# Three edits around the router of an expert layer: where eight weight loads stand in the queue, where three row scalings stand on VectorE, and forty products that nobody reads

## The chip, the cores and the metric

The kernel runs on one core of one Trainium2 chip. The metric is the device time of one execution in microseconds (us). TensorE is called PE in the rows (PEld is its weight load), VectorE is DVE, ScalarE is ACT, GpSimd is POOL, and SyncE is SP. A "q" behind an engine's name is its sequencer, which issues DMAs and takes branches.

## The reference

The model is a small float32 network of two parts. The first part has two layers. Each is a mixer (neighbourhood attention and an mLSTM in layer 0, grouped attention in layer 1) followed by a mixture of experts; a second part of two other layers follows. The change lies in the mixture of experts, which the reference computes as:

```python
scores = sigmoid(h @ router_w)                      # (N, 16)
sel = (scores + router_b).reshape(N, 4, 4)
g_idx = argmax(top_k(sel, 2)[0].sum(-1), -1)        # best group of four experts
e_idx = ...                                         # the best two experts inside that group
w = w / w.sum(-1)                                   # their scores, normalised
for e in range(16):
    y = y + comb[:, e:e+1] * ((silu(h @ w1[e]) * (h @ w3[e])) @ w2[e])
```

N is 512 tokens in layer 0 (256 latent and 256 context rows) and 256 tokens in layer 1; the width is 1024, an expert's inner width 512.

## The kernel before

**Products.** Each float32 weight is split in two numbers that PE multiplies faster: ACT copies it to a rounded `wh` (L90) and DVE subtracts to get the rest `wl` (L91). A product of weights and tokens is then three matmuls, `wh·xh`, `wl·xh`, `wh·xl` (L105 to L107). There are three buffers of `wh` and of `wl`, so these splits can run at most three pieces ahead of PE. An expert is 12 pieces of 512 KB: eight for w1 and w3, four for w2.

**Router.** While the mixer's last products run, `Routes.half` (L992 to L1011) transposes the tokens (L164), multiplies them with the router's weights (L1006), takes squares on ACT (L1009) and multiplies the tokens by rows `scales` on DVE (L1011), which gives the token rows `xT`. `moe` (L1404) then decides on DVE, in some thirty small operations that end with `both` (L1490, kept as `decided`): for each token, which two experts it goes to. PE sums `both` over the tokens (L1499: counts before each token); from these DVE makes `q` (L1503, places of the first expert's tokens) and `hot` (L1506, one 128 x 128 table of ones and zeros for each tile of 128 tokens, 4 tiles in layer 0 and 2 in layer 1).

**Token rows.** `rows_out(t)` (L1443 to L1448) makes the scaled rows of tile t on DVE (L1446, 128 x 1024) and has POOL store them to memory (`hd`). The first expert doesn't wait for that memory: PE multiplies the rows with `hot` (L1523), which puts the first expert's tokens in their places, and ACT and DVE split the sum in `xh` and `xl` (L156, L157). All later experts fetch their tokens from `hd` with an indirect DMA from POOL (`gather`, L1608) by the index `idx`, which DVE computes (L1676, L1677) from products of `slotb` and `rk` (L1544, L1546). A gathered tile is transposed by PE (L164) and split again. The factors of the tokens are summed by PE as well (L1709, from `wsr` and `slotb`), while the first expert runs.

**Weight places.** SP issues all weight loads, in order (L1569). Places for pieces are of four kinds: `rawm` (own buffers of `moe`, 16 in layer 0 and 17 in layer 1), `raw` (8, shared with the rest of the kernel), `rawr` (6, over the memory of `xT`), and in layer 1 `more` (2). Pieces are consumed in the order in which the places stand. The last argument but one of `moe` (`late`) names the `rawm` buffers that come behind `raw` in that order:

```python
late, early = [own[i] for i in late], [u for i, u in enumerate(own) if i not in late]
turn = [*(lambda u=u: u for u in more), *early, *[c.raw] * c.RAW, *late]
```

In layer 0 `late` is empty, in layer 1 it is (0, 1, 2, 3, 4). Each load on SP also waits for the one eight loads ahead of it.

**What sets the order.** Each engine works its instructions off in a fixed order, which a scheduler lays out when the kernel is built: by data, buffers and its own estimate of when an operand is there. `tc.issue_after(x)` keeps an instruction behind another one in that order; `split_w` (L73 to L92) is placed with high priority. Behind the first expert's start stands a branch that all engines take (L1327, L1328: the rare case that an expert has more than 128 tokens).

Of the kernel before, what the change touches and what calls it, by code (L numbers as in the profile page):

```python
# [13 lines left out]
AF = mybir.ActivationFunctionType  # L14
ALU = mybir.AluOpType
# [3 lines left out]
P = 128  # L19
# [7 lines left out]
class Core:  # L27
# [108 lines left out]
    def lin_feat2_halves(self, x, w):  # L136


        banks = [[self.acc().rearrange("p (j t) -> p j t", j=2) for _ in range(2)] for _ in range(2)]
        for half, j in ((0, 0), (0, 1), (1, 0), (1, 1)):  # L140
            rows = w[half * 512:(half + 1) * 512, j * 512:(j + 1) * 512]
            for k0, h, l in self.chunks(rows, 512):
                for i in range(4):
                    for k in range(2):
                        a = (h[:, k, i * P:(i + 1) * P], l[:, k, i * P:(i + 1) * P])
                        kk = 4 * half + k0 + k
                        self.mm3(banks[j][i // 2][:, i % 2, :], a, [v[:, kk, :] for v in x], i % 2 == 0 and kk == 0,
                                 kk == KD - 1)
            if half:
                yield j, banks[j]  # L150
# [11 lines left out]
    def transpose(self, out, in_):  # L162
        n = in_.partition_size() if hasattr(in_, "partition_size") else in_.shape[0]
        self.nc.tensor.transpose(out, in_, self.ident[:n, :n])  # L164

    def rsqrt_small(self, out, ms, n):

        self.nc.gpsimd.tensor_tensor(out, ms, self.mhalf[:, :n], op=ALU.pow)


class Stats:
# [24 lines left out]
    def settle(self):  # L196

        c, nc = self.c, self.c.nc
        for x in self.put_off:
            self.gather(x)  # L200
        for i, sq in self.sq.items():
            half = sq[:, :256]
            if sq.shape[1] > 256:
                last = nc.vector.tensor_tensor(half, half, sq[:, 256:], op=ALU.add)
            for t in range(2):
                nc.tensor.matmul(self.tot[:, i + t:i + t + 1], half[:, t * P:(t + 1) * P], c.ones[:, 0:1],
                                 start=self.fresh, stop=True, skip_group_check=True)
                self.fresh = False
                self.left[i + t] = 0
        self.put_off, self.sq = [], {}  # L210
        return last
# [720 lines left out]
class Routes:  # L932
# [64 lines left out]
    def half(self, t, j, bank):  # L997

        c, nc = self.c, self.c.nc
        x, r = self.segs[t // 2]  # L1000
        at = slice(t % 2 * P, t % 2 * P + P)
        for i in range(4):
            c.transpose(bank[:, i * P:(i + 1) * P], x[:, 4 * j + i, at])
        for i in range(4):
            k = 4 * j + i
            nc.tensor.matmul(self.lg[:, t * NE:(t + 1) * NE], x[:, k, at], self.rwB[:, r, k, :], start=t == k == 0,  # L1006
                             stop=k == KD - 1, skip_group_check=True)
        sq = c.const.tile([P, 512], F32, name="sq", tag="sq", bufs=3)
        nc.scalar.activation(sq, bank, AF.Square, accum_out=self.ss[:, t, j:j + 1])  # L1009
        v = lambda a: a.rearrange("t (p j) -> t p j", j=KD)  # L1010
        nc.vector.tensor_tensor(self.turned(self.xT[t], j), v(bank), v(self.scales[r][j]), op=ALU.mult)  # L1011

# [391 lines left out]
def moe(c, s, L, segs, mods, routes, yd, later, slots, late, more=()):  # L1404
# [3 lines left out]
    nc, tc, ins = c.nc, c.tc, c.ins  # L1408
# [11 lines left out]
    slot = mc[:, NE + 12:NE + 12 + P]  # L1420
# [19 lines left out]
    hd = c.dram.tile([T, D], F32, name=f"hd{L}")  # L1440
    xts = [s.tile([P, D], F32, name="xt", tag=tag) for tag in ("ye", "fhl" if nt > 2 else "xg0", "xg0", "xg1")[:nt]]

    def rows_out(t):  # L1443
        r = segs[t // 2][1]
        with tc.issue_after(decided):
            nc.vector.scalar_tensor_tensor(xts[t], routes.xT[t], rstd[:, t:t + 1], routes.shifts[r], op0=ALU.mult,  # L1446
                                           op1=ALU.add)
        nc.gpsimd.dma_start(hd[t * P:(t + 1) * P, :], xts[t])  # L1448
# [39 lines left out]
    g16 = lambda a: a.rearrange("p t (g e) -> p (t g) e", g=4)  # L1488
    fgb = fg.rearrange("p h b -> p (h b)").unsqueeze(2).to_broadcast((P, nt * 4, 4))
    decided = nc.vector.scalar_tensor_tensor(g16(both), rank, 1.5, fgb, op0=ALU.is_lt, op1=ALU.mult).ins  # L1490
    rows_out(0)
    for k in range(2):
        nc.vector.scalar_tensor_tensor(g16(oh[:, k]), rank, float(k), fgb, op0=ALU.is_equal, op1=ALU.mult)


    pp = c.ps()
    for t in range(nt + 1):
        for j in range(min(t + 1, nt)):
            nc.tensor.matmul(pp[:, t * NE:(t + 1) * NE], ub if j == t else ob, both[:, j, :], start=j == 0,  # L1499
                             stop=j == min(t, nt - 1), skip_group_check=True)  # L1500

    q0 = s.tile([P, nt], F32, name="q0")
    nc.vector.scalar_tensor_tensor(q0, pp[:, 0:nt * NE:NE], 1.0, both[:, :, 0], op0=ALU.add, op1=ALU.mult)  # L1503
    hot = s.tile([P, nt, P], F32, name="hot", tag="mtf")
    for t in range(nt):
        nc.vector.tensor_scalar(hot[:, t, :], slot, 1.0, q0[:, t:t + 1], op0=ALU.add, op1=ALU.is_equal)  # L1506
    for t in range(1, nt):
        rows_out(t)

    over = s.tile([P, 2], F32, name="over")  # L1510
    nc.vector.tensor_reduce(over[:, 0:1], pp[:, nt * NE:(nt + 1) * NE], axis=AX.X, op=ALU.max)
# [3 lines left out]
    xh, xl = (s.tile([P, KD, P], F32R, name=n, tag=n) for n in ("xh", "xl"))  # L1515
# [5 lines left out]
    for t in range(nt):  # L1521
        for k in range(KD):
            nc.tensor.matmul(pss[k // 4][:, k % 4 * P:(k % 4 + 1) * P], xts[t][:, k * P:(k + 1) * P], hot[:, t, :],  # L1523
                             start=t == k % 4 == 0, stop=t == nt - 1, skip_group_check=True)
# [17 lines left out]
    for n, (k, t) in enumerate((k, t) for k in range(2) for t in range(nt)):  # L1542
# [4 lines left out]
                         stop=n == 2 * nt - 1, skip_group_check=True)  # L1547
# [155 lines left out]
    for e in range(NE):  # L1703
        f, last = up(e, x, f)
        if e == 0:
            pw = c.ps()
            for a in range(2):
                for n, (b, k, t) in enumerate(sb):
                    nc.tensor.matmul(pw[:, :NE], b, wsr[:, a, k, t], start=a == n == 0, stop=a == 1 and n == 2 * nt - 1,  # L1709
                                     skip_group_check=True)  # L1710
# [10 lines left out]
        if e == NE - LATE:  # L1721
            rows_back()
            which = spare([P, LATE, T], F32R, "which")
            for i in range(LATE):
                for t in range(nt):
                    nc.vector.tensor_scalar(which[:, i, t * P:(t + 1) * P], slot, float(P * t), lastt[:, i:i + 1],
                                            op0=ALU.add, op1=ALU.is_equal)
# [18 lines left out]
    st = Stats(c)  # L1746
    banks = []
    with tc.issue_after(done[0].ins):
# [6 lines left out]
        for k in range(KD):  # L1755
# [5 lines left out]
            ps = banks[k]  # L1761
            for i, (x, r) in enumerate(segs):
                nc.vector.scalar_tensor_tensor(x[:, k, :], ps[:, 256 * i:256 * i + 256], mods.col(5, k, r), x[:, k, :],
                                               op0=ALU.mult, op1=ALU.add)
# [271 lines left out]
def program(tc, ins, out):  # L2036
    nc = tc.nc
    with ExitStack() as ctx:
        c = Core(tc, ctx, ins)
        xl = c.act.tile([P, KD, 256], F32, name="xl")  # L2040
        with ExitStack() as b1:
            c.b1 = b1.enter_context(c.tmp_pool(name="b1"))
            xc = c.b1.tile([P, KD, 256], F32, name="xc", tag="xc")
            with c.tmp_pool(name="even") as s:
# [14 lines left out]
                mods = [Mods(c, 0), Mods(c, 1)]  # L2059
# [22 lines left out]
                bank = lambda: c.st_p.tile([P, 512], F32, name="ada", tag="st")  # L2082
# [10 lines left out]
                B = lambda L: mods[L].scale("B", 4, gains[L][:, 8:16])  # L2093
                routes, yd = even_mixer(c, s, h, nMr, gq, xl, xc, mods[0], lambda: B(0), ada, first_w, made)
            with c.tmp_pool(name="moe0") as s:
                st = moe(c, s, 0, [(xc, 1), (xl, 0)], mods[0], routes, yd, False, 16, ())
            A = mods[1].scale("A", 1, gains[1][:, 0:8])
            with c.tmp_pool(name="odd") as s:
                routes, yd = odd_mixer(c, s, xl, xc, st, mods[1], A, lambda: B(1), ada)
            with c.tmp_pool(name="moe1") as s:  # L2100
                more = c.b1.tile([P, 2, 2, 512], F32, name="more", tag="xc")
                st = moe(c, s, 1, [(xl, 0)], mods[1], routes, yd, True, 17, (0, 1, 2, 3, 4), [more[:, i] for i in range(2)])
        xs = block2_consts(c, ctx.enter_context(c.tmp_pool(name="const2")))
        c.held = scaled(c, xs, xl, c.n1[:, 0, :], range(KD))[5:1:-2] + [c.early]
        for L in range(2):
            w = {n: ins[n][L] for n in W2}
            w["cols"], w["qkg"] = ins[f"cols_{L}"], ins[f"qkg_{L}"]
            xs, st = block2_layer(c, L, xl, xs, w, st, out if L == 1 else None)
# [31 lines left out]
```

## Time and profile before

| | us |
|---|---|
| median of 3 runs | 2318.12 (2313.27 to 2326.68) |
| the profiled execution | 2316.98 |
| its span, first to last instruction | 2315.2 |
| PE busy | 2222.4 (96%) |
| DVE busy | 1789.7 (77%) |
| ACT busy | 1505.2 (65%) |
| POOL busy | 152.3 (7%) |
| mean granted clock of PE | 0.982 |
| moved from memory | 498.39 MB |

A busy PE is not a PE at its peak, and idle time of an engine that isn't the bottleneck costs nothing. The expert layer of layer 0 starts at about 411 us of the span, that of layer 1 at about 904 us.

### The profile page before, as it was taken

What the parts mean: (1) busy time and instruction counts of PE and PEld (TensorE: products, weight loads), DVE (VectorE), ACT (ScalarE), POOL (GpSimd) and SP (SyncE); (2) the same over time, 40 slices, a digit from 0 to 9 for tenths busy, and PEclk for the clock granted to TensorE, in tenths of its full rate; (3) what the DMA queues carried; (4) which work ended last, traced back from release to release, by engine and by line L of the source; (5) the groups of instructions that cost most, each with busy time, mean ns of one, the idle gap of its engine ahead of it and who ended that gap; (6) DMA issues with size and microseconds to landing.
All of it is one profiled execution on the core that took longest, in us unless ns stands there. A gap on an engine that the chain in (4) does not pass through costs nothing.

```text
span 2315.2 us, 37957 instructions
## 1 busy us (share of the span) xinstructions
PE 2222.4 (96%) x14089; PEld 1887.8 (82%) x14089; DVE 1789.7 (77%) x2817; ACT 1505.2 (65%) x2398; POOL 152.3 (7%) x202
## 2 busy tenths in 40 slices
PE   8999999889999998999999999999999999999999
PEld 5665657767777667777778899999999899999997
DVE  4334743789989775899888999778976899867984
ACT  4333442478877453788776999656765999755773
POOL 0020000111110100111101100000000100000000
PEclk9999979899999999999999999999999999999999
DMA  8577603899993745999946545656666645656653
GB/s 303 170 242 279 204 26 118 312 347 366 365 336 142 270 167 207 377 398 348 325 148 204 177 136 150 190 182 183 194 201 185 184 139 146 186 178 183 192 184 117
DMA packets 206204, 507.24 MB, mean 219 GB/s; under 512 B 22711, under 2 KB 32335, under 8 KB 206008
## 3 DMA queue, kind: packets, MB, share of 16 engines
q1 hardware_dynamic: 196728, 490.08, 63.1%
q0 software_dynamic: 9280, 14.62, 1.7%
q8 instruction: 114, 1.87, 0.3%
q14 instruction: 82, 0.67, 0.1%
HBM read 498.39 MB, written 25.19 MB: 226 GB/s over the span
## 4 chain that ended last, share of the span: by engine, by line
PE 51%; DVE 10%; issue 8%; ACT 6%; DMA 3%; POOL 1%; DVEq 0%; SPq 0%; ACTq 0%; POOLq 0%
PE acc L106 15%; PE acc L107 15%; PE acc L105 14%; DVE wl L91 6%; ACT wh L90 3%; PE ps L164 2%; ACT cp L592 1%; DMA raw<-in_exp_w 1%; DMA rawm<-in_exp_w 1%; PE ps L1903 1%; DMA rawr<-in_exp_w 1%; ACT mtf L1635 1%; PE ps L451 0%; PE acc L1894 0%; DVE conf L597 0%
## 5 line engine op out<-in xcount | busy, mean ns | idle before, releaser
L91 DVE TENSOR_TENSOR wl<-raw,wh 128x1024 fp32r<-128x1024 f32 (+2 forms) x520 | 616.1, 1191 | 240.8 <-ACT wh L90 236.4
L90 ACT CAST wh<-raw 128x1024 fp32r<-128x1024 f32 (+2 forms) x520 | 532.1, 1026 | 356.1 <-PE acc L106 187.4
L106 PE MATMUL acc<-hl,wh 128*128 128x256 f32 (+1 forms) x1568 | 450.0, 287 | 0.3 <-DVE hl L916 0.3
L107 PE MATMUL acc<-hh,wl 128*128 128x256 f32 (+1 forms) x1568 | 450.0, 287 | 0.0
L105 PE MATMUL acc<-hh,wh 128*128 128x256 f32 (+1 forms) x1568 | 449.1, 287 | 0.7 <-ACT hh L913 0.6
L105 PEld LDWEIGHTS acc<-hh,wh 128*128 128x128 f32 x1568 | 295.5, 189 | 11.7 <-issue 4.2
L106 PEld LDWEIGHTS acc<-hl,wh 128*128 128x128 f32 x1568 | 295.9, 189 | 7.0 <-issue 2.5
L107 PEld LDWEIGHTS acc<-hh,wl 128*128 128x128 f32 x1568 | 294.9, 188 | 5.8 <-issue 1.3
L91 DVE TENSOR_TENSOR wl<-rawm,wh 128x1024 fp32r<-128x1024 f32 x210 | 250.9, 1219 | 17.6 <-ACT wh L90 14.2
L90 ACT CAST wh<-rawm 128x1024 fp32r<-128x1024 f32 x210 | 218.1, 1052 | 48.8 <-PE acc L107 45.9
L106 PE MATMUL acc<-wl,xh 128*128 128x512 f32 x512 | 211.5, 413 | 16.4 <-DVE wl L91 16.1
L105 PE MATMUL acc<-wh,xh 128*128 128x512 f32 x512 | 202.0, 399 | 6.3 <-PEq L1328 6.3
L107 PE MATMUL acc<-wh,xl 128*128 128x512 f32 x512 | 202.5, 395 | 0.0
L105 PE MATMUL acc<-bh,wh 128*128 128x256 f32 x640 | 178.6, 279 | 0.7 <-ACT bh L273 0.7
L106 PE MATMUL acc<-bl,wh 128*128 128x256 f32 x640 | 178.7, 279 | 0.4 <-DVE bl L274 0.4
L107 PE MATMUL acc<-bh,wl 128*128 128x256 f32 x640 | 178.7, 279 | 0.0
L592 ACT ACTIVATE cp<-ap,col 128x256 f32<-128x256 f32 x368 | 164.7, 506 | 6.4 <-DVE conf L597 6.4
L106 PE MATMUL acc<-wl,hh 128*128 128x512 f32 (+1 forms) x384 | 145.4, 379 | 2.2 <-DVE wl L91 1.9
L105 PE MATMUL acc<-wh,hh 128*128 128x512 f32 (+1 forms) x384 | 147.1, 383 | 0.0
L106 PEld LDWEIGHTS acc<-wl,xh 128*128 128x128 f32 x512 | 97.1, 190 | 60.6 <-DVE wl L91 41.0
L107 PE MATMUL acc<-wh,hl 128*128 128x512 f32 (+1 forms) x384 | 144.6, 377 | 0.0
L106 PEld LDWEIGHTS acc<-bl,wh 128*128 128x128 f32 x640 | 121.1, 189 | 0.8 <-DVE bl L274 0.8
(493 smaller groups left out, 4514.4 us busy)
## 6 DMA issues: line engine op xcount, KB each, us to landing
rawm<-in_exp_w SPq DMA_DIRECT2D x210, 512.0 KB, 6.9
raw<-in_w_in SPq DMA_DIRECT2D x152, 512.0 KB, 3.6
raw<-in_exp_w SPq DMA_DIRECT2D x96, 512.0 KB, 7.0
raw<-in_ada_w SPq DMA_DIRECT2D x80, 512.0 KB, 5.1
raw<-in_w_up SPq DMA_DIRECT2D x80, 512.0 KB, 3.7
rawr<-in_exp_w SPq DMA_DIRECT2D x66, 512.0 KB, 7.0
raw<-in_w_down SPq DMA_DIRECT2D x44, 512.0 KB, 4.4
raw<-in_even_w_in SPq DMA_DIRECT2D x24, 512.0 KB, 5.1
```

The lines of the kernel that those rows point to most:

```text
L90: nc.scalar.copy(h[:, :, :n], raw[:, :, :n])
L91: self.splits.append(nc.vector.tensor_tensor(l[:, :, :n], raw[:, :, :n], h[:, :, :n], op=ALU.subtract).ins)
L105: nc.tensor.matmul(out, a[0], b[0], start=start, stop=False, skip_group_check=True)
L106: nc.tensor.matmul(out, a[0], b[1], start=False, stop=False, skip_group_check=True)
L107: return nc.tensor.matmul(out, a[1], b[0], start=False, stop=stop, skip_group_check=True)
L164: self.nc.tensor.transpose(out, in_, self.ident[:n, :n])
L592: nc.scalar.activation(p[:, i, :], src[:, i, :], AF.Copy, scale=wv)
L1635: nc.scalar.activation(v, a, AF.Tanh, scale=0.5)
L1903: nc.tensor.matmul(po[:, :256], v[:, b, g0 * P:(g0 + 1) * P], pT[:, b].rearrange("p t q -> p (t q)"), start=b == 0, stop=b == 3)
```

## The change

There are three edits. First, layer 0 calls `moe` with `late` = (13, 14, 15): SP then loads 13 `rawm` pieces, the 8 `raw` pieces, the 3 other `rawm` pieces and the 6 `rawr` pieces, where it loaded 16, 8 and 6 before. Second, the scalings of token tiles 1 and up (`rows_out`) must come behind the last `hot` (`marked`), where they had to come behind `both` before. Third, PE gets 20 float32 products of the identity with itself, into a bank that nobody reads, placed behind the last square of the router's statistics; this holds for both layers.

```diff
+    def keep_on(self, n):
+        ps = self.ps("idle")
+        for _ in range(n):
+            self.nc.tensor.matmul(ps[:, :P], self.ident, self.ident, start=True, stop=True, skip_group_check=True)
...
-        nc.scalar.activation(sq, bank, AF.Square, accum_out=self.ss[:, t, j:j + 1])
+        self.seen = nc.scalar.activation(sq, bank, AF.Square, accum_out=self.ss[:, t, j:j + 1]).ins
...
-    def rows_out(t):
+    def rows_out(t, after):
         r = segs[t // 2][1]
-        with tc.issue_after(decided):
+        with tc.issue_after(after):
...
-    rows_out(0)
+    rows_out(0, decided)
...
+    with tc.issue_after(routes.seen):
+        c.keep_on(20)
     pp = c.ps()
...
     for t in range(nt):
-        nc.vector.tensor_scalar(hot[:, t, :], slot, 1.0, q0[:, t:t + 1], op0=ALU.add, op1=ALU.is_equal)
+        marked = nc.vector.tensor_scalar(hot[:, t, :], slot, 1.0, q0[:, t:t + 1], op0=ALU.add, op1=ALU.is_equal).ins
     for t in range(1, nt):
-        rows_out(t)
+        rows_out(t, marked)
...
-                st = moe(c, s, 0, [(xc, 1), (xl, 0)], mods[0], routes, yd, False, 16, ())
+                st = moe(c, s, 0, [(xc, 1), (xl, 0)], mods[0], routes, yd, False, 16, (13, 14, 15))
```

Lines of the changed kernel are 6 higher behind `keep_on` and 8 higher from L1500 on; the names of lines below are those of the kernel before.

**VectorE, layer 0, from `both` on.** Before:

```order
L1490 SCALAR_TENSOR_TENSOR both<-rank,fg 128x64
L1446 SCALAR_TENSOR_TENSOR xt<-xT,route,shifts 128x1024
L1493 SCALAR_TENSOR_TENSOR oh<-rank,fg 128x64 x2
L1503 SCALAR_TENSOR_TENSOR q_3459<-ps,both 128x4
L1446 SCALAR_TENSOR_TENSOR xt<-xT,route,shifts 128x1024
L1506 TENSOR_SCALAR hot<-mc,q_3459 128x128 x4
L1446 SCALAR_TENSOR_TENSOR xt<-xT,route,shifts 128x1024 x2
L1511 TENSOR_REDUCE over<-ps 128x1
L1529 TENSOR_TENSOR rk<-oh,mc 128x8x16
L1512 TENSOR_SCALAR over<-over 128x1
```

and now:

```order
L1496 SCALAR_TENSOR_TENSOR both<-rank,fg 128x64
L1452 SCALAR_TENSOR_TENSOR xt<-xT,route,shifts 128x1024
L1499 SCALAR_TENSOR_TENSOR oh<-rank,fg 128x64 x2
L1511 SCALAR_TENSOR_TENSOR q_3480<-ps,both 128x4
L1519 TENSOR_REDUCE over<-ps 128x1
L1514 TENSOR_SCALAR hot<-mc,q_3480 128x128 x4
L1452 SCALAR_TENSOR_TENSOR xt<-xT,route,shifts 128x1024 x3
L1520 TENSOR_SCALAR over<-over 128x1
L1537 TENSOR_TENSOR rk<-oh,mc 128x8x16
```

The four `hot` (L1506, now L1514) stand ahead of tile 1's scaling (`xt`) and behind one small operation (`over`); the other three scalings follow in one piece.

**VectorE, layer 0, the stretch that ends with `idx`.** It begins behind the split of the first expert's tokens (`xl`, L157). Before, the first row here is the first weight split (`wl`, L91) behind `xl`:

```order
L91 TENSOR_TENSOR wl<-rawm,wh 128x1024
L1544 TENSOR_SCALAR slotb<-mc,pk 128x128 x3
L1555 TENSOR_TENSOR den<-wk 128x4
L91 TENSOR_TENSOR wl<-rawm,wh 128x1024
L1556 RECIPROCAL den<-den 128x4
L91 TENSOR_TENSOR wl<-rawm,wh 128x1024
L1557 TENSOR_TENSOR wk<-wk,den 128x8
L1676 TENSOR_SCALAR none<-ps 128x32
L91 TENSOR_TENSOR wl<-rawm,wh 128x1024
L1558 TENSOR_TENSOR ws<-oh,wk 128x128
L91 TENSOR_TENSOR wl<-rawm,wh 128x1024
L1677 SCALAR_TENSOR_TENSOR idx<-ps,none 128x32
```

and now, where two weight splits and two pairs of `slotb` stand between `xl` and the first row here:

```order
L91 TENSOR_TENSOR wl<-rawm,wh 128x1024
L1552 TENSOR_SCALAR slotb<-mc,pk 128x128
L1563 TENSOR_TENSOR den<-wk 128x4
L91 TENSOR_TENSOR wl<-rawm,wh 128x1024
L1564 RECIPROCAL den<-den 128x4
L1684 TENSOR_SCALAR none<-ps 128x32
L1565 TENSOR_TENSOR wk<-wk,den 128x8
L91 TENSOR_TENSOR wl<-rawm,wh 128x1024 x2
L1566 TENSOR_TENSOR ws<-oh,wk 128x128
L91 TENSOR_TENSOR wl<-rawm,wh 128x1024
L1569 TENSOR_TENSOR wsr<-ws,wsr 128x128
L1685 SCALAR_TENSOR_TENSOR idx<-ps,none 128x32
```

Between `xl` and `idx` there are seven weight splits now, and five before, and the second half of `wsr` has come ahead of `idx`. In layer 1 there are five where there were three.

**ScalarE, layer 0, from the ninth expert's Tanh (`mtf`, L1635) to the tenth's.** Before:

```order
L1635 ACTIVATE mtf<-acc 128x128x4
L90 CAST wh<-rawm 128x1024 x3
L156 CAST xh<-ps 128x512
L90 CAST wh<-rawm 128x1024
L156 CAST xh<-ps 128x512
L90 CAST wh<-rawm 128x1024 x3
L1662 ACTIVATE ye<-acc,wsl 128x512 x2
L90 CAST wh<-raw 128x1024 x2
L159 ACTIVATE fhl<-ps 128x512
L90 CAST wh<-raw 128x1024 x2
L1635 ACTIVATE mtf<-acc 128x128x4
```

and now:

```order
L1643 ACTIVATE mtf<-acc 128x128x4
L90 CAST wh<-rawm 128x1024 x4
L156 CAST xh<-ps 128x512 x2
L90 CAST wh<-raw 128x1024 x3
L1670 ACTIVATE ye<-acc,wsl 128x512
L90 CAST wh<-raw 128x1024
L1670 ACTIVATE ye<-acc,wsl 128x512
L90 CAST wh<-raw 128x1024 x3
L159 ACTIVATE fhl<-ps 128x512
L90 CAST wh<-raw 128x1024
L1643 ACTIVATE mtf<-acc 128x128x4
```

Before, the splits of the gathered tokens (`xh`) come apart from each other in this stretch, as they do in all later experts; now they still stand together, as in the experts ahead of it, and come apart one expert later.

On PE, the 20 products stand in layer 0 between the last router products (L1006) and the first sum of `both` (L1499); in layer 1 18 stand there, and two among the last transposes of the router's tokens. The sums of the factors (L1709) all stand ahead of the first gathered tile's transposes now (16 in layer 0, 8 in layer 1), where half of them stood behind these before. POOL's order is unchanged.

## Rows read from the trace of the kernel before

**Rows 1.** The page: the chain of waits that ended last, by engine

```profile
PE 51%; DVE 10%; issue 8%; ACT 6%; DMA 3%; POOL 1%; DVEq 0%; SPq 0%; ACTq 0%; POOLq 0%
```

**Rows 2.** Timeline, PE, layer 0 (start us, us, operation, [idle before <-what ended it])

```profile
417.15 0.19 PE L1499 MATMUL ps<-both,ub 128*128 128x16 bf16 x1 [6.16 <-DVE both L1490]
...
420.17 9.82 PE L1523 MATMUL ps<-hot,xt 128*128 128x128 f32 x64 [2.48 <-DVE hot L1506]
...
445.16 1.38 PE L164 MATMUL ps<-ident,xg 128*128 128x128 f32 x8 [2.11 <-DMA xg<-hd,idx]
...
447.91 0.77 PE L105 MATMUL acc<-wh,xh 128*128 128x512 f32 x1
```

**Rows 3.** Timeline, DVE, layer 0

```profile
418.55 1.28 DVE L1446 SCALAR_TENSOR_TENSOR xt<-xT,route,shifts 128x1024 f32<-128x1024 f32 x1
419.75 0.96 DVE L1506 TENSOR_SCALAR hot<-mc,q 128x128 f32<-128x128 f32 x4
...
430.65 0.69 DVE L157 TENSOR_TENSOR xl<-ps,xh 128x512 fp32r<-128x512 f32 x1
...
438.95 0.18 DVE L1677 SCALAR_TENSOR_TENSOR idx<-ps,none 128x32 int32<-128x32 f32 x1
```

**Rows 4.** Timeline, PE, layer 1

```profile
912.66 5.78 PE L1523 MATMUL ps<-hot,xt 128*128 128x128 f32 x32 [2.82 <-DVE hot L1506]
...
933.33 1.44 PE L164 MATMUL ps<-ident,xg 128*128 128x128 f32 x8 [2.64 <-DMA xg<-hd,idx]
...
935.28 0.77 PE L105 MATMUL acc<-wh,xh 128*128 128x512 f32 x1
```

**Rows 5.** Windows, the products with `hot` alone: busy us (records), clock

```profile
420.20:424.80 4.60, 4.60 (x22) 4.60 (x23) 0.50 1.00 382
425.50:429.50 4.00, 4.00 (x39) 4.00 (x38) 1.00 1.02 419
```

**Rows 6.** Timeline, DVE, layer 1

```profile
919.10 0.69 DVE L157 TENSOR_TENSOR xl<-ps,xh 128x512 fp32r<-128x512 f32 x1 [0.20 <-ACT xh L156]
...
924.12 0.18 DVE L1677 SCALAR_TENSOR_TENSOR idx<-ps,none 128x32 int32<-128x32 f32 x1
```

**Rows 7.** Waits of SP from 360 to 520 us: total, times, longest

```profile
SPq L1569 <- DVE route L1018: 43.1, 1, 43.1
```

**Rows 8.** Windows with the share of the DMA engines

```profile
380.00:408.00 28.00, 0.45 (x2) 1.00 0.01 1
440.00:450.00 10.00, 4.05 (x3) 0.79 0.78 265
920.00:930.00 10.00, 3.40 (x3) 1.00 1.03 415
```

**Rows 9.** Timeline, SP: loads before and behind the branch, layer 0

```profile
421.51 10.91 SPq L1569 DMA_DIRECT2D rawr<-in_exp_w  x6
444.74 16.34 SPq L1569 DMA_DIRECT2D rawm<-in_exp_w  x16
```

**Rows 10.** Timeline, POOL: the first gather of layer 0, then of layer 1

```profile
439.97 1.10 POOL L1608 DMA_INDIRECT xg<-hd,idx  x1 [5.10 <-DVE lastt L1679]
...
925.08 1.43 POOL L1608 DMA_INDIRECT xg<-hd,idx  x1 [2.67 <-DVE idx L1677]
```

**Rows 11.** Timeline, ACT: Tanh of four experts, the eighth to the eleventh

```profile
576.86 1.12 ACT L1635 ACTIVATE mtf<-acc 128x512 f32<-128x512 f32 x1
...
595.44 1.12 ACT L1635 ACTIVATE mtf<-acc 128x512 f32<-128x512 f32 x1
...
612.89 1.13 ACT L1635 ACTIVATE mtf<-acc 128x512 f32<-128x512 f32 x1 [0.26 <-PE acc L107]
...
632.86 1.13 ACT L1635 ACTIVATE mtf<-acc 128x512 f32<-128x512 f32 x1 [0.68 <-PE acc L107]
```

**Rows 12.** The page: weight splits on DVE, busy us, mean ns | idle before

```profile
L91 DVE TENSOR_TENSOR wl<-rawm,wh 128x1024 fp32r<-128x1024 f32 x210 | 250.9, 1219 | 17.6 <-ACT wh L90 14.2
```

**Rows 13.** The branch's line, PE's own row: both layers, duration ns min/median/max

```profile
L1328 PEldq COMPARE_BRANCH  x2: 333/3310/6288, 469.2 to 959.2; - x2
```

## The prediction

> **What bounds the kernel.** I read the chain of waits on the page first. PE holds 51% of it and DVE and ACT 16%; DMA holds 3% and "issue" 8% [rows 1]. Weight loads are thus hardly ever what ends last, and a shorter load phase alone is worth little. The change touches the start of the two expert layers, so next I read the timelines of PE and DVE there. In layer 0 PE waits three times before its second expert: 6.16 us until the router has decided, 2.48 us until `hot` is there, and 2.11 us for the first gathered tile [rows 2]. The first of these waits stays: the router's arithmetic on DVE isn't touched. So at most the waits behind it, and the products that run slowly behind them, can shrink, and whatever shrinks must get past the gather.
>
> **Edit 2, `hot` ahead of the scalings.** In layer 0 `hot` begins 1.20 us behind the start of tile 1's scaling [rows 3]. That goes, less about 0.1 us for one small operation now ahead of it. The products with `hot` start at about 419.1 instead of 420.17. They don't wait for the scalings: tile 3 is scaled by about 419.6 + 3 x 1.20 = 423.2 us, and PE comes to it only behind three quarters of its records. Layer 1 is alike: 912.66 becomes about 911.5 [rows 4].
>
> **Edit 3, products without a reader.** Behind PE's idle time the products with `hot` began at a granted clock of 0.50, which is 1.2 GHz: 22 records in 4.60 us, 0.209 us each; at 1.00 (2.4 GHz) 39 ran in 4.00 us, 0.103 us each [rows 5]. These are float32 products of 128 x 128, as the new ones are, and come as two records each (32 products in layer 0, 64 records). So the 20 new ones are 40 records: 40 x 0.103 = 4.1 us at full clock, 40 x 0.209 = 8.4 us at half. PE is free at 417.15 - 6.16 = 411.0 us; they end at 415.1, or 419.4 at worst. The first lies under the wait for the router and costs nothing; the second would hold up the sums of `both` by 2.3 us. I take the first, since the clock fell only during the idle time. But PE then still idles 2 us before the sums and another 1.4 us before `hot`, so they need not keep the clock. If it stays full, the 64 products take 64 x 0.103 = 6.6 us for 9.82, and the first expert starts 1.1 + 3.2 = 4.3 us earlier; if it falls as before, 1.1 us. In layer 1, 32 x 0.103 = 3.3 for 5.78, thus 1.2 to 3.7 us; two of the new products stand among the router's transposes there and may cost 4 x 0.103 = 0.4 us.
>
> **What is late next: the gather.** PE waits for it already [rows 2, 4], and nothing in the edits brings it forward by itself. It is released by `idx`, on a DVE that works in order, and there the order has become worse: seven weight splits instead of five stand between `xl` and `idx` in layer 0, five instead of three in layer 1. A split there takes its turn when PE frees a buffer. From the end of `xl` (430.65 + 0.69) to `idx` (438.95) five splits and the small operations took 7.61 us, 1.52 us for each [rows 3]. Seven are 10.65 us. With `xl` 1.1 to 4.3 us earlier, `idx` starts at 437.7 to 440.9: between 1.3 us earlier and 1.9 us later than before; the middle is 0.3 later. In layer 1 three took 4.33 us [rows 6], 1.44 each; five are 7.2 us, with `xl` 1.2 to 3.7 us earlier, so 0.8 earlier to 1.7 later, middle 0.4 later. The first expert's gain is thus spent on DVE's order.
>
> **Behind the gather.** From the first gathered tile's transposes to the next weight product PE took 2.75 us in layer 0, where eight sums of factors stood between, and 1.95 us in layer 1, where four did [rows 2, 4]. These move ahead, into PE's wait, so 0 to 0.8 us are gained in layer 0 and 0 to 0.3 in layer 1; I take 0.4 and 0.2.
>
> **Edit 1, eight loads earlier.** SP waited 43.1 us, until DVE had read the last scale rows, on a `rawm` load [rows 7], and all that time the DMA engines were idle: share 0.01 at 380 to 408 us [rows 8]. The eight `raw` pieces (4 MB, about 10 us at 415 GB/s) now go there. PE doesn't wait for them, so the direct gain is nothing. What they trigger: the six `rawr` loads, which SP could issue only over 421.51 to 432.42 us because each waits for the load eight ahead, are out by about 426 us, when the branch's own operand is ready. SP is then past the branch 12.3 us later (432.42 to 444.74 before [rows 9]), at about 438, and issues loads into the `rawm` places that the first expert has freed. Before, the gather of layer 0 met a queue that ran dry: 439.97 to the transposes at 445.16, 5.2 us [rows 2, 10], with a DMA share of 0.78 at 440 to 450 us [rows 8]. In layer 1, with a share of 1.03 around the gather, the same took from 925.08 to 933.33, 8.25 us [rows 4, 8, 10]. So the gather of layer 0 costs 0 to 3.06 us more. I take the middle, 1.5: the loads start just before the gather, not well before it as in layer 1.
>
> The Trainium skill says in "DMA: Bandwidth & Descriptors" (Issuing engines are not separate DMA queues) that DMAs of all issuing engines run on the same 16 DMA engines and interleave. By that POOL's gather has no lane of its own beside SP's loads, which speaks against this edit; the two gathers just named, 5.2 and 8.25 us, agree. By that rule alone the full 3.06 us would be the value and the time 1.5 us longer.
>
> **The splits' order.** From the tenth expert on, `xh` of the gathered tokens comes in two parts, and an expert takes 632.86 - 612.89 = 19.97 us, where the ninth took 595.44 - 576.86 = 18.58 [rows 11]. In the changed order this switch comes one expert later in layer 0: 1.4 us gained. In layer 1 it stays.
>
> **Sum.** Layer 0: 0.3 - 0.4 + 1.5 = +1.4 us, bounds -1.3 - 0.8 = -2.1 and 1.9 + 3.06 = +5.0. Switch: -1.4. Layer 1: 0.4 - 0.2 + 0.2 = +0.4, bounds -1.1 and +2.1. In all +0.4 us, bounds -4.6 and +5.7. The profiled execution took 2316.98 us (span 2315.2 and 1.8 around it), 1.1 us under the median of the three runs. 2317.4 by that execution, 2318.5 by the median: I forecast 2318 us. A change under 0.5%, 11.6 us, can't be told from none here.
>
> **Rivals.**
>
> *The gain carries through* (0.15). DVE has slack before `idx`, and the seven splits take less than 1.52 us each because PE starts them earlier, at full clock: at 1.22 us, their own length [rows 12], they are 8.5 us and `idx` comes about 3.4 us earlier in layer 0 and 1.9 in layer 1, with the gather as before. With the switch and the sums -8 us, 2310 us. For it: PE's waits for the first gathered tiles are short. Against: the splits were paced by PE, not by their length.
>
> *The branch moves* (0.15). PE stood still for 6.3 us at the branch in layer 0 and 0.3 us in layer 1 [rows 13], for no data. The new products shift all PE instructions behind them. If the stall in layer 0 goes, that is -6 us, 2312 us (0.10). If layer 1 gets one, +6, 2324 us (0.05). The branch is the same code in both layers, which speaks for chance; that nothing else in the row differs speaks for no change. The Trainium skill, in "Runtime: NRT & Kernel Launch" (Instruction fetch mechanics), says that a taken branch whose target isn't in the instructions already loaded waits for a DMA. By that rule the stall would depend on where the code lies, as this rival has it; no row here shows where it lies.
>
> *Slower: the gather behind the loads* (0.15). SP passes the branch by 438 us and fills the queues, and the gather of layer 0 lands in 8.25 us or more while `idx` comes 1.9 us later. This decides if the clock falls again, so that the first expert starts only 1.1 us earlier. Price: the upper bound, +5.7 us, 2323 us.
>
> *The new products don't do what they say* (0.05). They run at half clock and hold up the sums of `both` by 2.3 us in layer 0: with the rest 2320 us.
>
> **Chances.** My forecast, within 4 us of 2318, has 0.50. All single cases lie within 0.5%; faster than that needs two of them at once (gain carried and stall gone, -14, 2304 us), slower needs the late gather with a new stall (+12, 2330 us). With the spread of the runs I say 0.15 faster, 0.77 same, 0.08 slower. Range 2307 to 2327 us; the forecast's own is 2313 to 2323.
>
> **What would show it.** Right: the products with `hot` begin 1.1 us behind their old distance from `both`; `idx` starts within 2 us of its old distance from `both`; the first gather takes over 5.2 us in layer 0, with a DMA share near 1; PE's wait for the first gathered tile is longer than 2.1 us. The 40 records should end before the sums of `both`. Wrong: the second expert starts over 3 us earlier, measured from `both`, in either layer; the stall at the branch comes or goes; PE waits for weight pieces.

## The result and the profile after

The changed kernel takes 2332.52 us (median of 10 runs, 2323.12 to 2344.74), the kernel before 2314.46 us (10 runs, 2308.36 to 2326.68). The ratio is 1.0079, 95% interval 1.0056 to 1.0103: slower by 13 to 24 us, where I had forecast 2318 us and no change. The profiled execution took 2328.57 us. Three lines of its page:

```profile
span 2326.8 us, 38107 instructions
PE 2234.8 (96%) x14169; PEld 1899.0 (82%) x14169; DVE 1791.7 (77%) x2817; ACT 1505.3 (65%) x2398; POOL 152.7 (7%) x202
PE 39%; issue 7%; DVE 7%; ACT 5%; POOL 1%; DMA 0%; DVEq 0%; ACTq 0%; POOLq 0%
```

The span is 11.6 us longer than before. PE is busy 12 us longer, 11 of them with the new products (6.07 us in layer 0 and 5.04 in layer 1), which mostly lie in what were waits. Where the time went is read from the Tanh of the experts on ACT (start, length), here those of the first three experts of layer 0 and of the second and third of layer 1. Before:

```profile
437.65 1.12 ACT L1635 ACTIVATE mtf<-acc 128x512 f32<-128x512 f32 x1
457.24 1.12 ACT L1635 ACTIVATE mtf<-acc 128x512 f32<-128x512 f32 x1
484.18 1.12 ACT L1635 ACTIVATE mtf<-acc 128x512 f32<-128x512 f32 x1
...
943.42 1.10 ACT L1635 ACTIVATE mtf<-acc 128x512 f32<-128x512 f32 x1
965.49 1.15 ACT L1635 ACTIVATE mtf<-acc 128x512 f32<-128x512 f32 x1
```

and after (lines are 8 higher):

```profile
431.63 1.13 ACT L1643 ACTIVATE mtf<-acc 128x512 f32<-128x512 f32 x1
454.88 1.11 ACT L1643 ACTIVATE mtf<-acc 128x512 f32<-128x512 f32 x1
485.68 1.12 ACT L1643 ACTIVATE mtf<-acc 128x512 f32<-128x512 f32 x1
...
948.61 1.10 ACT L1643 ACTIVATE mtf<-acc 128x512 f32<-128x512 f32 x1
976.06 1.12 ACT L1643 ACTIVATE mtf<-acc 128x512 f32<-128x512 f32 x1
```

From the second to the third Tanh, layer 0 took 26.9 us and takes 30.8, layer 1 took 22.1 and takes 27.5: +3.9 and +5.4 us, four fifths of the loss in two stretches. Both contain the branch. PE's own row of the branch, which read 333 and 6288 ns before [rows 13], is now:

```profile
L1334 PEldq COMPARE_BRANCH  x2: 5928/6018/6107, 465.8 to 964.4; - x2
```

So layer 1 has a wait of 6.1 us where it had 0.3. In layer 0 the wait was there before; what is new is a second one just behind it, 1.99 us (last row below). PE's timeline of layer 0 after, with what answers to [rows 2]:

```profile
408.32 6.07 PE L170 MATMUL idle<-ident 128*128 128x128 f32 x40
...
415.62 7.38 PE L1531 MATMUL ps<-hot,xt 128*128 128x128 f32 x64 [0.89 <-DVE hot L1514]
...
445.27 1.94 PE L164 MATMUL ps<-ident,xg 128*128 128x128 f32 x8 [7.23 <-DMA xg<-hd,idx]
...
471.86 0.77 PE L107 MATMUL acc<-wh,fhl 128*128 128x512 f32 x1 [5.73 <-PEq L1334]
...
477.18 0.79 PE L105 MATMUL acc<-wh,xh 128*128 128x512 f32 x1 [1.99 <-ACT wh L90]
```

The first expert does start sooner: counted from `both` on DVE (416.87 before, 413.38 after) the products with `hot` begin 2.2 us later instead of 3.3, and take 7.38 instead of 9.82 us, 3.5 us gained (of these, 2.4 us were this execution's clock, as two later traces show). All of it goes into the wait for the first gathered tile, 7.23 us for 2.11. DVE, POOL and SP show why (answering to [rows 3], [rows 10], [rows 9] and [rows 7]):

```profile
413.38 0.22 DVE L1496 SCALAR_TENSOR_TENSOR both<-rank,fg 128x64 bf16<-128x64 f32 x1
...
436.33 0.18 DVE L1685 SCALAR_TENSOR_TENSOR idx<-ps,none 128x32 int32<-128x32 f32 x1
```

```profile
437.35 1.27 POOL L1616 DMA_INDIRECT xg<-hd,idx  x1 [5.00 <-DVE idx L1685]
```

```profile
410.16 6.24 SPq L1577 DMA_DIRECT2D raw<-in_exp_w  x8
...
423.15 11.15 SPq L1577 DMA_DIRECT2D rawr<-in_exp_w  x6
445.13 12.58 SPq L1577 DMA_DIRECT2D rawm<-in_exp_w  x13
```

```profile
SPq L1577 <- DVE route L1024: 46.7, 1, 46.7
```

`idx` comes 22.95 us behind `both` instead of 22.08, and its gather takes 7.9 us to PE's transposes (437.35 to 445.27) instead of 5.2. SP's rows hold a surprise: the eight `raw` loads were not moved into the idle time. SP still waited 46.7 us for the scale rows ahead of them, now at the eleventh load and not at the fourteenth; the changed `moe` takes the three late places from memory first, so the eleventh to thirteenth place, not the late ones, came to lie over the scale rows. The share of the DMA engines at 380 to 408 us is 0.00.

### The profile page after: what moved, and what is told of

Read it like the earlier page. It is cut to its first block, busy times and chain, and to the rows that moved or that the text cites. A ratio compares the mean times of both kernels' runs of the same rounds, so it can differ in the third digit from the quotient of the medians.

```text
span 2326.8 us, 38107 instructions
## 1 busy us (share of the span) xinstructions
PE 2234.8 (96%) x14169; PEld 1899.0 (82%) x14169; DVE 1791.7 (77%) x2817; ACT 1505.3 (65%) x2398; POOL 152.7 (7%) x202
## 3 DMA queue, kind: packets, MB, share of 16 engines
q8 instruction: 115, 1.88, 0.3%
## 4 chain that ended last, share of the span: by engine, by line
PE 39%; issue 7%; DVE 7%; ACT 5%; POOL 1%; DMA 0%; DVEq 0%; ACTq 0%; POOLq 0%
PE acc L106 12%; PE acc L107 12%; PE acc L105 12%; DVE wl L91 3%; ACT wh L90 2%; ACT cp L598 2%; PE ps L164 1%; PE ps L457 0%; DVE conf L603 0%; ACT ta L501 0%; POOL rs L174 0%; PE ps L515 0%; ACT mtf L1643 0%; DVE conf L600 0%; PE ps L492 0%
## 5 line engine op out<-in xcount | busy, mean ns | idle before, releaser
L91 DVE TENSOR_TENSOR wl<-raw,wh 128x1024 fp32r<-128x1024 f32 (+2 forms) x520 | 616.5, 1192 | 233.6 <-ACT wh L90 228.7
L91 DVE TENSOR_TENSOR wl<-rawm,wh 128x1024 fp32r<-128x1024 f32 x210 | 251.2, 1220 | 27.5 <-ACT wh L90 24.3
```

The costliest lines, as they stand in the source:

```text
L91: self.splits.append(nc.vector.tensor_tensor(l[:, :, :n], raw[:, :, :n], h[:, :, :n], op=ALU.subtract).ins)
```

## The experiments

The theory after this reading (A): PE waits at the branch for its own code, and how long depends on where that code lies; the new products shift it. PE's loads of code can be counted on the page: q8 moved 115 packets, 1.88 MB, 16 KB each, and PE ran 2 x 14169 instructions, 246 for each packet. (The kernel before has 114 packets; the kernel `after_aligned` below, with 520 instructions of PE more, has 116.) The last such packet before the branch of layer 1 stands at 953.3 us in the trace before and at 939.1 us in the changed one. From there to the branch PE ran, before (columns: stretch, busy us and records of PE, PEld, DVE, ACT, POOL, then clock, DMA share, GB/s):

```profile
953.30:959.20 5.90, 5.90 (x27) 4.59 (x26) 5.48 (x6) 4.35 (x5) 0.00 (x0) 1.00 1.02 410
```

and after:

```profile
939.15:964.40 25.25, 25.01 (x107) 19.97 (x106) 21.01 (x21) 18.04 (x21) 1.98 (x2) 0.91 0.87 329
```

That is 53 instructions against 213: the 160 added ones (40 products, each two records of PE and two of PEld). And in the changed kernel a packet of code moves during the wait (DMA of 964.4 to 970.6 us), and again during the second wait of layer 0 (474.9 to 475.1 us):

```profile
q8 instruction: 1, 0.02, 1.0%
...
q8 instruction: 1, 0.02, 29.2%
```

All thirteen traces below agree. At each of their 16 long waits at the branch one packet of q8 starts 3.4 to 3.8 us behind the branch's start, and the wait ends 2.4 to 2.6 us behind the packet's start. In the four traces with a second wait in layer 0, PE goes on 2.2 to 2.3 us behind the start of the next packet. The profile puts the second wait down to ACT (`wh`) in the changed kernel, but that split had ended at 476.32 us, 0.86 us before PE went on.

Rivals: (B) the order of the loads makes gather and weights late; (C) the products cost the time themselves. Each kernel below `after` was timed in five rounds against the kernel before (12 executions, but 10 of `only_idle` and 6 of `before_pad`), in three groups on three chips, each group beside its own executions of the kernel before. The table has the ratio with its interval, PE's wait at the branch in layers 0 and 1, the time from the second to the third Tanh there, and PE's wait for the first gathered tile.

| kernel | ratio | branch, us | 2nd to 3rd Tanh, us | gather, us |
|---|---|---|---|---|
| before | 1 | 6.3 / 0.3 | 26.9 / 22.1 | 2.1 / 2.6 |
| after | 1.0079 (1.0056 to 1.0103) | 5.9 / 6.1 | 30.8 / 27.5 | 7.2 / 3.0 |
| only_late | 1.0015 (0.9994 to 1.0037) | 5.8 / 0.3 | 26.3 / 22.1 | 5.3 / 2.6 |
| only_hot | 1.0005 (0.9984 to 1.0026) | 6.1 / 0.3 | 26.7 / 22.1 | 4.2 / 3.6 |
| only_idle | 1.0051 (1.0025 to 1.0077) | 5.9 / 5.9 | 31.4 / 27.3 | 0.7 / 3.5 |
| before_pad | 1.0091 (1.0056 to 1.0126) | 5.9 / 6.1 | 29.5 / 28.2 | 2.6 / 2.7 |
| after_pad1 | 1.0043 (1.0022 to 1.0064) | 5.9 / 0.3 | 30.9 / 22.1 | 4.9 / 3.2 |
| after_aligned | 1.0020 (0.9997 to 1.0044) | 6.0 / 0.3 | 26.2 / 22.0 | 5.6 / 3.1 |
| no_idle | 1.0028 (1.0007 to 1.0049) | 5.8 / 0.3 | 26.3 / 22.1 | 4.9 / 3.6 |
| late_own_place | 1.0013 (0.9995 to 1.0031) | 5.9 / 0.3 | 26.6 / 22.1 | 5.0 / 2.5 |
| before_idx | 0.9975 (0.9950 to 1.0001) | 6.0 / 0.3 | 27.0 / 22.0 | 0 / 0.7 |
| aligned_idx | 1.0005 (0.9981 to 1.0029) | 5.9 / 0.3 | 27.0 / 21.5 | 1.7 / 0 |
| hot_idx | 0.9993 (0.9967 to 1.0020) | 6.0 / 0.3 | 26.7 / 22.1 | 0 / 0 |

**Each edit alone.** `only_late` is the kernel before with the one line

```diff
-                st = moe(c, s, 0, [(xc, 1), (xl, 0)], mods[0], routes, yd, False, 16, ())
+                st = moe(c, s, 0, [(xc, 1), (xl, 0)], mods[0], routes, yd, False, 16, (13, 14, 15))
```

> The kernel before with the first edit alone (13 rawm pieces, 8 raw, 3 rawm, 6 rawr). In the changed kernel's trace SP still waited 46.7 us on DVE's read of the scale rows, now on the eleventh load instead of the fourteenth, so the raw pieces were not earlier. Theory A (the loss is the branch, where PE waits for its own code): this edit moves no PE instruction, so 0 within 2 us, and the wait in layer 1 at the branch stays 0.3 us. Theory B (the order of the loads makes gather and weights late): +5 us or more here. Theory C (the products without a reader cost the time): 0.

Measured: 1.0015, no difference that can be told, and neither stretch at the branch is longer. B falls for the loss as a whole. It holds for the gather alone: that took 8.4 us here, and PE waited 5.3 us for it.

`only_hot` has the edit of `rows_out` and `marked` alone:

```diff
-        with tc.issue_after(decided):
+        with tc.issue_after(after):
...
-        rows_out(t)
+        rows_out(t, marked)
```

> The kernel before with the second edit alone (scalings of tile 1 and up behind the last hot). Theory A: in layer 0 the branch stands four products earlier on PE, inside the last products of expert 1, as in the changed kernel, which took 3.9 us more there from expert 1's to expert 2's Tanh (30.8 for 26.9 us); so +2 to +4 us, no new wait at the branch in layer 1 (0.3 us). If instead the branch's place in layer 0 is harmless, -1 to -3 us from the earlier start of the first expert. Theory B and C: 0 or -1.

Measured: 1.0005. The branch does stand four products earlier in layer 0, and that is harmless: 26.7 us. This part of my theory was wrong.

`only_idle` has `keep_on(20)` alone:

```diff
+    with tc.issue_after(routes.seen):
+        c.keep_on(20)
     pp = c.ps()
```

> The kernel before with the third edit alone (20 products without a reader in each expert layer). Theory A: PE's code behind them lies 80 instructions further in layer 0 and 160 in layer 1, so that in layer 1 the branch's target is no longer loaded when PE gets there: PE waits about 6 us at the branch in layer 1 (0.3 before), expert 1's to expert 2's Tanh takes about 27.5 us there (22.1 before), +5 us in all, less 1 to 2 us from the clock. Theory B: 0. Theory C: +8 us or more, but from the products' own time or the clock and not at the branch.

Measured: 1.0051, the wait in layer 1 is there (5.9 us), and layer 0 has its long stretch too (31.4 us). So both belong to this edit. A and C are not yet apart.

**The same number of instructions with little work.** `before_pad` has, in place of the 20 float32 products, 40 small ones:

```diff
+    with tc.issue_after(routes.seen):
+        pad_ps = c.ps("idle")
+        for _ in range(40):
+            nc.tensor.matmul(pad_ps[:, :NE], ob, ob[:, :NE], start=True, stop=True, skip_group_check=True)
```

> The kernel before with 40 small bf16 products (128x16) without a reader in each expert layer where the 20 float32 ones stand in the changed kernel: the same number of PE instructions (two each, 80 in a layer), but only about 1.2 us of PE's time, inside its wait for the router. Theory A: the wait at the branch in layer 1 appears as in only_idle, about 6 us, and the kernel is 5 us slower. Theory B and C: 0 within 2 us, no wait at the branch in layer 1.

Measured: 1.0091, with 1.2 us of added work in either layer. PE's row of the branch in it:

```profile
L1328 PEldq COMPARE_BRANCH  x2: 5888/6008/6127, 468.7 to 961.3; - x2
```

C falls for the waits: they come not from what the products do, but from how many instructions they are. The two stretches account for 2.6 + 6.1 = 8.7 us; the interval begins at 13 us, so 4 us or more of this kernel's loss are not explained by its trace. That trace is of the fastest of its six executions, 2319.29 us (median 2336.56), only 2.3 us longer than the profiled one of the kernel before.

**Code shifted on.** `after_pad1` is the changed kernel with 48 more of the small products in layer 1:

```diff
+    if L == 1:
+        with tc.issue_after(routes.seen):
+            pad_ps = c.ps("idle")
+            for _ in range(48):
+                nc.tensor.matmul(pad_ps[:, :NE], ob, ob[:, :NE], start=True, stop=True, skip_group_check=True)
```

> The changed kernel with 48 more small bf16 products without a reader in layer 1 alone, inside the wait for the router: PE's code at layer 1's branch then lies 256 instructions behind its place in the kernel before instead of 160. The rows of code that PE fetches in the traces are 16 KB each, 256 instructions of 64 bytes. Theory A (the wait at the branch depends on where the code lies in such pieces): the wait in layer 1 falls back from 6.1 to 0.3 us, expert 1's to expert 2's Tanh there from 27.5 to 22.1 us, layer 0 stays as in the changed kernel: 1.005 of the kernel before, where the change has 1.008. Rival (any added PE instruction costs, wherever it lies): 1.008 or more, wait still there.

Measured: 1.0043, though PE has 96 instructions more than the changed kernel (the two intervals still overlap, 1.0056 to 1.0064). Its branch row:

```profile
L1334 PEldq COMPARE_BRANCH  x2: 343/3140/5937, 465.9 to 966.1; - x2
```

The wait of layer 1 is gone, and the second wait of layer 0 (2.00 us) stays, since only layer 1's code was moved. `after_aligned` does both:

```diff
-        c.keep_on(20)
+        pad_ps = c.ps("idle")
+        for _ in range(132 if L == 0 else 128):
+            nc.tensor.matmul(pad_ps[:, :NE], ob, ob[:, :NE], start=True, stop=True, skip_group_check=True)
```

> The changed kernel with its 20 float32 products replaced by 132 small bf16 products in layer 0 and 128 in layer 1, about 4 us of PE's time in either, as before, but 264 and 256 instructions: the code at both branches then stands 256 and about 520 instructions behind the kernel before, so at the same place (within 8 instructions) in a piece of 256. Theory A: no wait at the branch in layer 1; in layer 0 one wait of 6 us and no second one behind it, expert 1's to expert 2's Tanh 26.9 us (30.8 in the changed kernel) and 22.1 us in layer 1; what is left of the change is the longer wait for the first gather, +1 to +3 us, less 1.4 us: ratio 0.999 to 1.001. Rival (products without a reader cost by themselves, by clock or queue): 1.005 or more.

Measured: 1.0020. Both stretches are back to 26.2 and 22.0 us; with all three edits in place and 3.7 and 3.4 us of products without a reader, what is left of the loss can't be told from none, and the interval lies below that of the changed kernel.

**Edits 1 and 2, and edit 1 as it was meant.** `no_idle` is the changed kernel without `c.keep_on(20)`:

```diff
-    with tc.issue_after(routes.seen):
-        c.keep_on(20)
```

> The changed kernel without the products without a reader: edits 1 and 2 together. Theory A: PE's code moves by 8 instructions at most, no wait in layer 1, layer 0 as in only_hot (26.7 us from expert 1's to expert 2's Tanh): 1.000 to 1.002. Rival (edits 1 and 2 together make the gather late enough to matter, though neither does alone): 1.003 or more.

Measured: 1.0028, clear of 1 but between the two expectations and so undecided; the sum of `only_late` and `only_hot` would be 1.0020. `late_own_place` is `only_late` with the late places taken from memory last:

```diff
-    first = [u() for u in late]
+    first = [u() for u in late] if more else []
...
-    places = itertools.chain(turn[:-len(late) or None], ((lambda u=u: u) for u in first), last,
+    places = itertools.chain(turn[:-len(late) or None], ((lambda u=u: u) for u in first) if more else late, last,
```

> The kernel before with edit 1, but with the three late places taken from memory behind the other thirteen, so that they, and not the eleventh to thirteenth place, lie over the scale rows. SP's wait for DVE's read of these rows then stands behind the eight raw loads, as the prediction had it: the raw pieces should land at 386 to 400 us, while the DMA engines were idle (share 0.01), and SP should be past the branch some 6 us sooner. Theory A: PE doesn't wait for these pieces, and the gather of layer 0 meets more loads: 0 to +3 us, ratio 1.000 to 1.001. Rival (loads ten us earlier free the DMA engines later and are worth their time): -3 us or more, ratio 0.998.

Measured: 1.0013. Now the loads do go into the idle time, as SP's timeline and the DMA share at 380 to 408 us (last but one column) show:

```profile
377.43 17.76 SPq L1569 DMA_DIRECT2D raw<-in_exp_w  x8
420.85 1.28 SPq L1569 DMA_DIRECT2D rawm<-in_exp_w  x3
428.36 5.76 SPq L1569 DMA_DIRECT2D rawr<-in_exp_w  x6
```

```profile
380.00:408.00 28.00, 28.00 (x144) 1.00 0.59 231
```

Nothing is gained by it: the rival falls, and PE waits 5.0 us for the gather, which took 8.1 us.

**What a sooner `idx` is worth.** Three kernels give the two operations that make `idx` priority, in the kernel before (`before_idx`), in `after_aligned` (`aligned_idx`) and with edit 2 alone (`hot_idx`):

```diff
-    nc.vector.tensor_scalar(none, po[:, :2 * NE], 0.0, float(1 << 20), op0=ALU.is_equal, op1=ALU.mult)
-    nc.vector.scalar_tensor_tensor(idx, po[:, :2 * NE], -1.0, none, op0=ALU.add, op1=ALU.add)
+    with tc.high_priority():
+        nc.vector.tensor_scalar(none, po[:, :2 * NE], 0.0, float(1 << 20), op0=ALU.is_equal, op1=ALU.mult)
+        nc.vector.scalar_tensor_tensor(idx, po[:, :2 * NE], -1.0, none, op0=ALU.add, op1=ALU.add)
```

> The kernel before with the two DVE operations that make idx given priority in the order, so that two or three weight splits fewer stand ahead of them; the code at the branches moves by two instructions. Theory: PE's wait for the first gathered tile (2.1 us in layer 0, 2.6 in layer 1) is set by DVE's order, so idx comes 3 to 4 us sooner and both waits go: -3 to -5 us, ratio 0.998 to 0.999. Rival (the gather lands behind the weight loads, whenever it is issued): 0.

> after_aligned with idx given priority in the same way. PE waits 5.6 us (layer 0) and 3.1 us (layer 1) for the first gathered tile there, since the first expert starts sooner and idx doesn't. Theory (the gain of edits 2 and 3 is real and is lost behind idx): the wait in layer 0 falls below 3 us, in layer 1 below 1.5 us: -4 to -6 us against after_aligned, ratio to the kernel before 0.998 to 1.000. Rival (the gather takes the longer the earlier it is issued, since it then meets more loads): as after_aligned, 1.002.

> Edit 2 alone with idx given priority: no products without a reader, loads as before, code at both branches where it stood before. Theory: the first expert starts 1.1 us sooner, the wait for the first gathered tile (4.2 us in layer 0 and 3.6 in layer 1 in only_hot) falls by about 3 us in each: ratio 0.997 to 0.999, the best of these kernels. Rival as for before_idx: 1.000.

Measured: 0.9975, 1.0005 and 0.9993, none clear of 1. The waits for the first gathered tile shrank or went, so DVE's order sets them; but in part another wait came in their place. `wsr`, which the sums of the factors need, is made behind `idx` in this order, and PE waits for it, here in layer 0 of `before_idx`:

```profile
446.56 1.06 PE L1710 MATMUL ps<-wsr,slotb 128*128 128x16 f32 x8 [1.38 <-ACT wsr L1560]
```

The same wait took 1.5 us in layer 0 of `hot_idx` and `aligned_idx`, and 1.3 and 3.4 us in layer 1 of the two. So next to nothing was gained in layer 0 of `before_idx`: the transposes of the first gathered tile begin 28.1 us behind `both` (28.3 before), the clock fell to 0.50 behind the wait as it did before, and the second Tanh came 19.4 us behind the first (19.6). In layer 1 PE waited only 0.7 us for the tile, the clock stayed at 1.00, and the second Tanh came 2.7 us sooner behind the first (15.2 for 17.9 us).

In layer 0 of `after_aligned`, with its long wait, the stretch at half clock lay mostly over the wait: 0.50 and no record from 446 to 449 us, 1.00 from 452 us on. In `aligned_idx`, with the wait for the tile down to 1.7 us, the clock was 0.50 from 455 to 464 us, with PE busy throughout (one trace, of an execution 17 us over the median of its kernel). So my theory for `aligned_idx` fell: the tile came 2.5 us sooner behind `both` in layer 0, and the time stayed. `before_idx` is the best of these kernels, but its interval ends at 1.0001.

## Why the prediction was wrong

**The step that failed** is the branch, which the sum put at nothing. I gave a new wait in layer 1 a chance of 0.05 (the rival "The branch moves"), since the same code in both layers seemed to speak for chance, though the change itself says how many instructions it adds. The coming or going of that stall was one of my own signs of being wrong, and it came. The rival priced the new wait at +6 us (measured +5.4 between the Tanh) and missed that layer 0 would get a second wait (2 to 3.8 us in four kernels) and more time at half clock, together +3.9. That makes +9.3 of the 11.8 us by which the two expert layers are longer in the profiled execution. `before_pad`, `after_pad1` and `after_aligned` show the cause, one by making it, two by taking it away. The Trainium skill ("Runtime: NRT & Kernel Launch", Instruction fetch mechanics) has a taken branch wait for a DMA where its target isn't loaded, and this agreed with the traces: a packet of code moves during each long wait.

**Edit 1** failed as well, and harmlessly: I let the loads go into the idle time, and they didn't. As `late_own_place` shows, it wouldn't have helped.

**The gather** was right in its mechanism and too small in size. `idx` came 0.9 us later behind `both` (I took 0.3, bounds -1.3 to 1.9): the seven splits took 11.3 us, where I had 10.65. The gather took 2.7 us more (I took 1.5, bound 3.06), but not because SP's next loads went out sooner: they went out later (445.13 against 444.74, with `both` 3.5 us earlier), and the DMA engines were still full at 438 to 443 us (share 1.02), with the late loads of `rawr` just issued. In all, from `both` to the first gathered tile 28.3 became 31.9 us, +3.6 (I took +1.8 for these two terms). The other traces split this. With edit 1 alone `idx` comes as before (22.2 us behind `both`), but the gather takes 8.4 us: 31.6 us to the tile. With edit 2 alone `idx` comes at 25.1 us, 3.1 later than before and beyond my bound, and the gather takes 4.9 us: 31.0 us. With both edits, and `idx` not moved, it is 31.8 to 32.2 us in four traces: the two delays don't add.

**The half clock** took some of that back. From the transposes of that tile to the second Tanh it was 12.1 us and is 9.6: the longer wait had swallowed part of the slow stretch (granted clock at 448 to 453 us 0.54 before, 0.93 after). I had 0.4 us there, for the sums. From `both` to the second Tanh layer 0 is thus 1.1 us longer and layer 1 1.5 us, against my +1.4 and +0.4.

**The products with `hot`** start 1.1 us sooner, as worked out, in every kernel with edit 2. That the new products hold the clock for them is not shown. In the changed kernel the 64 records of layer 0 took 7.38 us at a granted clock of 1.00 (0.115 us each). `only_idle` and `after_pad1` have the same new products there, and `hot` took 9.80 and 10.18 us, at 0.74 and 0.71, as without them (9.82). In layer 1 of the changed kernel the 32 records took 5.44 us at 0.69 (5.78 before). These are the three rows:

```profile
415.87 9.80 PE L1531 MATMUL ps<-hot,xt 128*128 128x128 f32 x64 [2.51 <-DVE hot L1514]
...
415.84 10.18 PE L1536 MATMUL ps<-hot,xt 128*128 128x128 f32 x64 [1.44 <-DVE hot L1519]
...
915.29 5.44 PE L1531 MATMUL ps<-hot,xt 128*128 128x128 f32 x32 [1.77 <-DVE hot L1514]
```

In the changed kernel's trace the clock was at 0.50 when the new products began and rose while they ran; in the other two it was full under them (4.7 us) and fell during `hot`. So the early first expert of that one trace was luck. The new products took 6.1 us there and not 4.1, and ended 0.6 us behind `both`, whose sums waited for them; `hot` came no later for it.

**The switch of the splits' order** was worth nothing: from the eighth to the eleventh Tanh it takes 55.9 us (18.57, 18.98, 18.36) for 56.0, where I had -1.4. I had misread [rows 11]: the three stretches before were 18.58, 17.45 and 19.97 us, and I set the longest against the first and left out the short one between them.

**What stays open.** By the ratio the loss is 13 to 24 us, by the two profiled executions 11.6, of which 11.8 lie in the expert layers and the rest cancels. What lies ahead of them varies from one execution to the next: `both` of layer 0 was at 412.6 to 425.4 us in these thirteen traces. One trace for each kernel can't say whether the code's place costs time elsewhere too. One place behind layer 0 does differ between the kernels: the mixer of layer 1, about 108 us behind the sixteenth Tanh (stretch, busy us and records of PE, clock, DMA share, GB/s; before, then after):

```profile
840.00:848.00 8.00, 7.76 (x37) 1.00 0.00 0
...
841.00:849.00 8.00, 7.22 (x23) 0.79 0.00 0
```

The clock fell there in all five kernels with edit 2 and `idx` where it was (`after`, `only_hot`, `after_pad1`, `after_aligned`, `no_idle`) and in none of the other eight. From the sixteenth Tanh to `both` of layer 1 the five took 179.7 to 182.4 us and the eight 177.2 to 179.1. So edit 2 seems to cost 2.3 to 5.0 us there against the kernel before (177.4); why is not shown.

## What to carry to other kernels

Instructions that are added to an engine shift all of its code behind them, and a branch further on can then wait 6 us for its target; so count the instructions to the branch and look at the trace's packets of code before an edit is judged by what it does. When a kernel that adds work is slower, run it once with the same number of idle instructions instead. A gain ahead of a wait is worth nothing until what sets the wait is moved too; then the next operand may be the late one, and a slow clock that the wait had hidden may come to lie over work. And read a gain in more than one trace: of two kernels with the same code in layer 0, one had its products at full clock and the other did not.

## What the runs showed that I had not expected

The wait at a taken branch was 5.8 to 6.3 us or 0.3 us, nothing between, in 13 kernels. In layer 1 it was 0.3 us with 50 to 64 instructions since the last packet of code and 5.9 to 6.1 us with 206 to 214, for the same jump. The jump of layer 0, whose skipped code handles four tiles of tokens and not two, always waited, with 10 to 30 instructions in nine kernels and with 79 to 90 in the four that have the second wait. Ninety-six more instructions took the wait of layer 1 away and made the kernel no slower (1.0043 for 1.0079).
